# Projections with features first, undivided attention weights, and an earlier end of attention in a two-layer trunk on one core

## The chip, the core and the metric

One core of a Trainium2 chip runs the whole program. TensorE (PE) multiplies, VectorE (DVE), ScalarE (ACT) and GpSimd (POOL) work on tiles, and SyncE (SP) issues most of the DMAs. The metric is the time of the program on the device in microseconds, as the median of several runs. The profile comes from one more execution.

## The reference

The reference is a trunk of two layers over one sequence of 1024 tokens with 1024 features, in float32. Layer 0 mixes tokens with a diagonal state-space model, layer 1 with sparse attention; each mixer is followed by an MLP with squared ReLU (4096 hidden features), with a norm before and behind each.

```python
def dsa_mixer(h, w_in, w_out):
    proj = h @ w_in
    q, k, v, qi, ki, wi = jnp.split(proj, offs, axis=-1)   # 16 heads, 4 of k and v, 8 of the indexer, 64 wide
    q, k, qi, ki = (apply_rope(...) for each)
...
    rel = jax.nn.relu(jnp.einsum('bthd,bsd->bths', qi_blk, ki))
    score = jnp.einsum('bths,bth->bts', rel, wi_blk)       # causal
    _, idx = lax.top_k(score, 256)                         # per query, over 1024 keys
    att = jnp.einsum('btngd,btknd->btngk', qg, kg) * scale # chosen keys alone
    p = jax.nn.softmax(att, axis=-1)
    o = jnp.einsum('btngk,btknd->btngd', p, vg)
...
    return out @ w_out

def sq_relu_mlp(h, w1, w2):
    a = jax.nn.relu(h @ w1)
    return (a * a) @ w2
```

## The kernel before

**Layout and precision.** The residual stream lies with features on the partitions, 512 tokens (half a sequence, `hf` 0 or 1) along a row. To keep float32 accuracy each operand x is held as a rounded part `hi` and a rest `lo = x - hi`; `mm3` (lines 138 to 143) makes three matmuls of each product. A weight unit (`unit`, line 111) is a DMA of 512 KB into one of three raw buffers, two ScalarE copies (line 123) and two subtractions (line 124, one on VectorE, one on GpSimd).

**Passes.** The state-space layer comes first. Then four passes of the MLP follow, one for each layer and half, in `run` (line 1138): layer 0 half 0 alone; layer 0 half 1 with the attention of the first half beside it (`first`); layer 1 half 0 with the attention of the second half beside it (`second`); layer 1 half 1 alone. A pass has 64 units of 24 matmuls with 512 columns. After each unit `beside` (line 266) takes `self.per` steps from the generator beside it: 5 in the second pass, after a wait of 8 units, and `PER_B` in the third. Between the second and third passes stand the output projection of the first half, a residual and norm, and the indexer's projections of the second half, with nothing of the MLP beside them.

**Order.** The program order is that of the Python calls, but a planner orders the instructions of each engine by its own estimate of when each is needed; the side work has a higher priority. Tiles with the same tag share a fixed number of buffers: 22 tiles of 4 KB a partition under the tag `b`, three raw buffers `wr` for all weights. Since raw buffers are handed out in program order, the place of a `unit` call among the MLP's units is kept. The output projection of the second half (`att_out`, line 1057) is called once 58 units are through:

```python
            while self.units < HOLD_OUT:
                yield
            xo = self.att_in(self.od[1], "b")
            yield from self.att_out(xo, "b")
```

**Projections.** `proj` (line 725) multiplies with tokens on the output partitions: the stationary operand is 128 tokens of x, the moving one 256 features of a weight chunk. `heads` (line 768) rotates the result with `apply_rope` (line 752: line 760 over 512 elements, 762 and 763 over 256, then two additions on GpSimd), splits it into hi and lo, and later transposes each head of each 128 tokens (line 782), so that hi and lo of 64 features fill the 128 partitions. ScalarE copies them out (lines 798, 811) and queries go to DRAM as `qd` and `qi` (line 799), 256 KB at a time. Keys stay in four tiles of 256 tokens. `index` makes two chunks of indexer queries (the first half only its last 256 tokens), `projections` four chunks of queries, then keys, then values.

**Attention.** A block `i` is 128 queries. `topk` (line 902) finds each query's 256th largest score by 31 bit steps, whose small instructions on VectorE (lines 946 to 960) alternate with counts on VectorE or ScalarE (lines 916, 954). Per head, `weights` (line 996) multiplies queries and keys in pieces of 256 keys (line 1013), adds the mask and takes the maximum (line 1015), scales the maximum (line 1017), takes the exponential with its sum (line 1019), inverts the sum (line 1020) and multiplies all weights by it on GpSimd (line 1021). `outputs` (line 1025) transposes the weights, splits them and multiplies with the values; the result goes to DRAM as `od` (line 1050). `att_in` (line 1054) loads it and splits it.

## Time and profile before

| | before |
|---|---|
| median of 3 runs | 2305.07 us (2303.75 to 2305.22) |
| the profiled execution | 2311.69 us, its span 2309.9 us |
| mean granted clock of TensorE | 0.976 |
| busy: TensorE, VectorE, ScalarE, GpSimd | 95%, 63%, 48%, 39% |
| data moved by DMA | 258.48 MB, 112 GB/s |

The span runs from the first to the last instruction. Times in the rows count from its start. Matmuls overlap, so a mean duration of one is more than the time from one start to the next.

### The profile page before, as it was taken

Reading aid. Unit: us, or ns where it says so; the run is one execution under the profiler, and the core shown is the slowest. Engines: PE = TensorE matmul, PEld = TensorE weight load, DVE = VectorE, ACT = ScalarE, POOL = GpSimd, SP = SyncE. Lnnn points to the kernel's source line nnn. Section 1 sums busy time; section 2 is a strip of 40 time slices with the busy share of each in tenths; the row PEclk is TensorE's granted clock in tenths of the full one; section 3 lists DMA queues with packets and bytes.
Section 4 is the critical chain, followed back from the end, with each engine's and each line's share of the span. In section 5 each row is a group of like instructions: output and inputs, shape, how many; then the busy total and the mean of one; then the engine's idle time right before and its main releaser. Section 6 shows DMA issues by size and latency. Waiting matters only on the chain.

```text
span 2309.9 us, 31616 instructions
## 1 busy us (share of the span) xinstructions
PE 2194.5 (95%) x11392; PEld 1844.8 (80%) x11392; DVE 1451.1 (63%) x2977; ACT 1097.7 (48%) x2003; POOL 889.4 (39%) x712
## 2 busy tenths in 40 slices
PE   7899999999999999999998989899999998999996
PEld 3577778888889987888888878777889887788886
DVE  9465953333653598566695899999766748333335
ACT  4435643333454465455464565665455544323332
POOL 6004542222346443344346424344545425222223
PEclk9899999999999999999999999999999999999998
DMA  6112442333345544443445424332333245433331
GB/s 245 55 30 80 163 138 94 101 93 99 115 134 162 143 120 107 115 109 108 149 165 147 137 91 101 83 82 78 87 87 89 73 137 178 133 99 99 94 101 54
DMA packets 92989, 258.48 MB, mean 112 GB/s; under 512 B 10912, under 2 KB 23584, under 8 KB 92832
## 3 DMA queue, kind: packets, MB, share of 16 engines
q1 hardware_dynamic: 79072, 232.34, 31.5%
q0 software_dynamic: 12672, 23.07, 5.4%
q8 instruction: 90, 1.47, 0.3%
q10 hardware_dynamic: 1088, 1.05, 0.1%
q14 instruction: 67, 0.55, 0.1%
HBM read 222.73 MB, written 32.51 MB: 110 GB/s over the span
## 4 chain that ended last, share of the span: by engine, by line
PE 72%; DVE 15%; issue 5%; ACT 5%; POOL 1%; DMA 0%; SPq 0%; DVEq 0%; ACTq 0%; POOLq 0%
PE m L141 17%; PE m L143 17%; PE m L142 17%; PE p L1013 2%; PE p L141 2%; PE p L143 2%; PE p L142 2%; PE p L1034 2%; DVE wh L124 1%; DVE b L234 1%; PE p L1043 1%; DVE b L191 1%; PE p L1042 1%; PE p L883 1%; DVE acc L234 1%
## 5 line engine op out<-in xcount | busy, mean ns | idle before, releaser
L142 PE MATMUL m<-b,wh 128*128 128x512 f32 (+1 forms) x2208 | 860.7, 391 | 9.7 <-DVE b L191 7.2
L141 PE MATMUL m<-b,wh 128*128 128x512 f32 (+1 forms) x2208 | 862.7, 392 | 6.8 <-DVE ring L1017 2.5
L143 PE MATMUL m<-b,wh 128*128 128x512 f32 (+1 forms) x2208 | 860.0, 391 | 3.4 <-DVE wh L124 3.4
L124 POOL TENSOR_TENSOR wh<-wr,wh 128x512 fp32r<-128x512 f32 x318 | 467.1, 1470 | 1004.9 <-ACT wh L123 962.3
L123 ACT ACTIVATE wh<-wr 128x512 fp32r<-128x512 f32 x636 | 396.4, 628 | 486.8 <-PE m L143 406.0
L142 PEld LDWEIGHTS m<-b,wh 128*128 128x128 f32 x2208 | 419.0, 190 | 93.1 <-DVE b L191 9.7
L141 PEld LDWEIGHTS m<-b,wh 128*128 128x128 f32 x2208 | 418.9, 190 | 92.2 <-issue 4.2
L143 PEld LDWEIGHTS m<-b,wh 128*128 128x128 f32 x2208 | 418.7, 190 | 86.4 <-DVE wh L124 3.8
L124 DVE TENSOR_TENSOR wh<-wr,wh 128x512 fp32r<-128x512 f32 x318 | 269.3, 848 | 307.3 <-ACT wh L123 284.4
L318 DVE TENSOR_TENSOR acc<-acc,m 128x512 f32<-128x512 f32 x216 | 147.0, 681 | 145.4 <-PE m L143 143.8
L1021 POOL TENSOR_TENSOR s<-s,ring 128x128 f32<-128x128 f32 (+7 forms) x128 | 157.8, 1244 | 160.3 <-DVE ring L1020 141.6
L283 ACT ACTIVATE b<-m 128x512 f32<-128x512 f32 x128 | 76.3, 596 | 154.6 <-PE m L143 153.9
L141 PE MATMUL p<-wh,b 128*128 128x256 f32 x480 | 136.1, 289 | 3.0 <-ACT wh L123 3.0
L142 PE MATMUL p<-wh,b 128*128 128x256 f32 x480 | 137.2, 290 | 1.7 <-POOL wh L124 1.4
L132 DVE CAST b<-b 128x1024 fp32r<-128x1024 f32 x68 | 60.9, 896 | 122.0 <-ACT b L285 117.7
L143 PE MATMUL p<-wh,b 128*128 128x256 f32 x480 | 135.9, 287 | 0.0
L1038 ACT ACTIVATE pt<-p 128x512 fp32r<-128x512 f32 (+1 forms) x160 | 83.5, 554 | 92.1 <-PE p L1034 90.1
L1015 DVE CUSTOM_DVE_ANT_0 s<-p,nb 128x512 f32<-128x512 f32 (+3 forms) x192 | 100.2, 549 | 31.8 <-PE p L1013 30.3
L1019 ACT ACTIVATE s<-s,ring 128x128 f32<-128x128 f32 (+7 forms) x128 | 98.6, 772 | 44.4 <-DVE ring L1017 40.5
L1039 DVE TENSOR_TENSOR pt<-p,pt 128x512 fp32r<-128x512 f32 (+1 forms) x160 | 98.9, 630 | 29.0 <-ACT pt L1038 28.6
L954 ACT ACTIVATE junk<-b,ring 128x512 bf16<-128x512 f32 (+2 forms) x90 | 80.7, 897 | 73.6 <-DVE ring L950 68.0
L1013 PE MATMUL p<-kt,q 128*128 128x256 f32 x640 | 104.9, 293 | 5.0 <-DVE acc L318 2.4
(295 smaller groups left out, 3090.6 us busy)
## 6 DMA issues: line engine op xcount, KB each, us to landing
wr<-in_w_dram SPq DMA_DIRECT2D x256, 512.0 KB, 3.6
wr<-in_wa_dram SPq DMA_DIRECT2D x32, 512.0 KB, 3.7
q<-qd POOLq DMA_DIRECT2D x64, 256.0 KB, 5.4
ld<-hd SPq DMA_DIRECT2D x24, 512.0 KB, 6.3
hd<-b SPq DMA_DIRECT2D x16, 512.0 KB, 4.5
qd<-qt SPq DMA_DIRECT2D x32, 256.0 KB, 3.4
wr<-in_wao_dram SPq DMA_DIRECT2D x16, 512.0 KB, 3.6
q<-qi POOLq DMA_DIRECT2D x24, 256.0 KB, 5.1
```

The costliest lines, as they stand in the source:

```text
L123: nc.scalar.activation(hi, r, AF.Copy)
L124: (nc.gpsimd if h else nc.vector).tensor_sub(lo, r, hi.bitcast(F32))
L141: mm(ps, w[0], x[0], start=start, stop=False)
L142: mm(ps, w[0], x[1], start=False, stop=False)
L143: return mm(ps, w[1], x[0], start=False, stop=stop)
L318: nc.vector.tensor_add(acc[d][:, j], acc[d][:, j], ps)
L1013: nc.tensor.matmul(ps[:, 256 * e:256 * e + 256], qt[:, v, 2 * hp + k, :], self.K[2 * c + e][:, g, :], start=v == 0, stop=v == 1)
L1015: nc.vector.tensor_tensor_reduce(out=s[:, a:a + n], in0=ps[:, :n], in1=nb[:, a:a + n], scale=1.0, scalar=-BIG, op0=ALU.add, op1=ALU.max, a ...
L1019: nc.scalar.activation(s, s, AF.Exp, bias=ng[:, k, 0:1], scale=0.125, accum_out=sm[:, k, 0:1])
L1021: nc.gpsimd.tensor_tensor(s, s, rc[:, k, 0:1].to_broadcast([128, W]), op=ALU.mult)
L1038: nc.scalar.activation(ph[:, :nk], pt[:, :nk], AF.Copy)
L1039: nc.vector.tensor_sub(pl[:, :nk], pt[:, :nk], ph.bitcast(F32)[:, :nk])
```

## The change

- Queries and keys are projected with features on the output partitions (`proj_f`): the stationary operand is 128 features, the moving one 512 tokens. The weights are reordered while they are split, so that the first halves of four heads stand before their second halves (`unit(..., heads=True)`). `turned` rotates with tables that `att_r` makes once per half: copies of cosine and sine, eight transposes, copies back.
- `put_heads` sends hi and lo of each head to DRAM with eight DMAs per 128 features. Keys take the same way (`kd`) and come back as tiles of 512 keys; they are made ahead of the queries. `weights` multiplies with up to 512 keys at once.
- The weights are no longer divided by their sum. The negative scaled maximum comes from one instruction per piece; the sums of a block's 16 heads are inverted, turned and sent to DRAM (`norms`), and `att_in` multiplies the outputs by them, broadcast from DRAM over 64 partitions.
- `PER_B` becomes (7, 6, 7, 6, 6) and the output projection of the second half follows attention after two holds of one unit (`WAIT_OUT`) and no longer waits for unit 58.

```diff
-PER_B = (8, 6, 10, 10, 10)
+PER_B = (7, 6, 7, 6, 6)
-HOLD_OUT = 58
+WAIT_OUT = 1
...
-            nc.scalar.activation(hi, r, AF.Copy)
-            (nc.gpsimd if h else nc.vector).tensor_sub(lo, r, hi.bitcast(F32))
             out.append((hi, lo))
+            if heads:
+                rs = r.rearrange("p (k h e d) -> p e k h d", h=2, e=2, d=32)
+                his, los = [q.rearrange("p (k e h d) -> p e k h d", h=2, e=2, d=32) for q in (hi, lo)]
+                parts = [(his[:, e], los[:, e], rs[:, e]) for e in range(2)]
+            else:
+                parts = [(hi, lo, r)]
+            for ph, pl, pr in parts:
+                nc.scalar.activation(ph, pr, AF.Copy)
+                (nc.gpsimd if h else nc.vector).tensor_sub(pl, pr, ph.bitcast(F32))
...
+    def proj_f(self, x, chunk, n, body):
+        pss = [self.p1([128, 512]) for _ in range(2)]
+        for u in range(2):
+            ws = self.unit(self.a["wa"][chunk, u], heads=True)
+            for h in range(2):
+                for m in range(2):
+                    for kk in range(2):
+                        kt = 4 * u + 2 * h + kk
+                        w = [t[:, 256 * kk + 128 * m:256 * kk + 128 * m + 128] for t in ws[h]]
+                        self.mm3(pss[m][:, n], w, [q[:, kt % 2, n] for q in x[kt // 2]], kt == 0, kt == 7)
+                    if u and h:
+                        body(m, pss[m][:, n])
+                yield
...
+    def turned(self, ps, n):
+        nc = self.nc
+        cos, sin = self.turns[:, 0, n], self.turns[:, 1, n]
+        w = ps.shape[-1]
+        b = self.blk([128, 2, 512], tag="b")
+        t1, t2 = b[:, 0, :w], b[:, 1, :w]
+        nc.vector.tensor_mul(t1, ps, cos)
+        nc.vector.tensor_mul(t2[0:64], ps[64:128], sin[64:128])
+        nc.vector.tensor_mul(t2[64:128], ps[0:64], sin[0:64])
+        nc.gpsimd.tensor_add(t1, t1, t2)
+        st = self.blk([128, 2, 512], F32R, tag="b")[:, :, :w]
+        nc.scalar.activation(st[:, 0], t1, AF.Copy)
+        nc.gpsimd.tensor_sub(st[:, 1], t1, st.bitcast(F32)[:, 0])
+        return st.bitcast(F32)
+
+    def put_heads(self, st, dst, h0, t0=0):
+        for e in range(2):
+            for v in range(2):
+                for h in range(2):
+                    src = st[64 * e + 32 * h:64 * e + 32 * h + 32, v]
+                    self.nc.sync.dma_start(
+                        dst[t0:, 64 * v + 32 * e:64 * v + 32 * e + 32, h0 + h].rearrange("t d n -> d t n"),
+                        src.rearrange("d (t n) -> d t n", n=dst.shape[-1]))
+
+    def queries(self, hf, x, chunk, dst, g, n=slice(0, 512)):
+        yield from self.proj_f(x, chunk, n, lambda m, ps: self.put_heads(
+            self.turned(ps, n), dst[4 * hf:4 * hf + 4], 4 * g + 2 * m, n.start // 128))
 
     def keys(self, hf, x):
+        n = slice(0, 512)
+        def body(m, ps):
+            self.put_heads(self.turned(ps, n), self.kd[hf:hf + 1], 2 * m)
+            kt = self.blk([128, 2, 512], F32R, name="kt")
+            self.nc.sync.dma_start(kt.bitcast(F32), self.kd[hf, :, 2 * m:2 * m + 2])
+            self.K[hf].append(kt)
+        yield from self.proj_f(x, 0, n, body)
...
-        mx, ng, sm, rc = [self.small([128, 2, 2], F32, "sf", 16) for _ in range(4)]
         for k, s in enumerate(P):
+            least = None
             for c in range(nk):
                 a, n = 512 * c, min(512, W - 512 * c)
+                m = max(n, 256)
                 ps = self.p1([128, 512])
-                for e in range((n + 255) // 256):
-                    for v in range(2):
-                        nc.tensor.matmul(ps[:, 256 * e:256 * e + 256], qt[:, v, 2 * hp + k, :],
-                                         self.K[2 * c + e][:, g, :], start=v == 0, stop=v == 1)
-                nc.vector.tensor_tensor_reduce(out=s[:, a:a + n], in0=ps[:, :n], in1=nb[:, a:a + n], scale=1.0,
-                                               scalar=-BIG, op0=ALU.add, op1=ALU.max, accum_out=mx[:, k, c:c + 1])
-            nc.vector.tensor_scalar(ng[:, k, 0:1], mx[:, k, 0:1], mx[:, k, nk - 1:nk], -0.125,
-                                    op0=ALU.max, op1=ALU.mult)
-            nc.scalar.activation(s, s, AF.Exp, bias=ng[:, k, 0:1], scale=0.125, accum_out=sm[:, k, 0:1])
-            nc.vector.reciprocal(rc[:, k, 0:1], sm[:, k, 0:1])
-            nc.gpsimd.tensor_tensor(s, s, rc[:, k, 0:1].to_broadcast([128, W]), op=ALU.mult)
+                for v in range(2):
+                    nc.tensor.matmul(ps[:, :m], qt[:, v, 2 * hp + k, :], self.K[c][g // 2][:, g % 2, :m],
+                                     start=v == 0, stop=v == 1)
+                last, least = least, self.small([128, 1], F32)
+                nc.vector.tensor_tensor_reduce(out=s[:, a:a + n], in0=ps[:, :n], in1=nb[:, a:a + n], scale=-0.125,
+                                               scalar=last if c else BIG, op0=ALU.add, op1=ALU.min, accum_out=least)
+            h = 16 * (i % 4) + 4 * g + 2 * hp + k
+            nc.scalar.activation(s, s, AF.Exp, bias=least, scale=-1.0, accum_out=self.sums[:, h:h + 1])
             yield
...
+    def norms(self, i):
+        r = self.sums[:, 16 * (i % 4):16 * (i % 4) + 16]
+        nc.vector.reciprocal(r, r)
+        ps = self.p1([16, 128])
+        nc.tensor.transpose(ps, r, self.ident)
+        t = self.small([64, 256], F32, "ot", 2)[0:16, 0:128]
+        nc.scalar.activation(t, ps, AF.Copy)
+        nc.sync.dma_start(self.rd[i // 4][:, i % 4], t)
...
-        return [self.split(b(), [128, 2, 512], lo_pool=j % 2 == 1, tag=tag) for j, b in enumerate(self.load_h(od))]
+    def att_in(self, hf, tag, wait=0):
+        nc, got = self.nc, []
+        for j, b in enumerate(self.load_h(self.od[hf])):
+            hi, lo = [self.blk([128, 2, 512], F32R, tag=tag) for _ in range(2)]
+            x, rb = b(), lo.bitcast(F32)
+            for q in range(2):
+                h = 4 * (2 * (j // 2) + q) + 2 * (j % 2)
+                nc.sync.dma_start(rb[64 * q:64 * q + 64],
+                                  self.rd[hf][h:h + 2].rearrange("(o h) t n -> o (h t n)", o=1).to_broadcast([64, 1024]))
+            got.append((x, hi, lo))
+            if j == 2:
+                yield from self.hold(wait)
+        for x, hi, lo in got:
+            nc.vector.tensor_mul(x, x, lo.bitcast(F32))
+            nc.scalar.activation(hi, x, AF.Copy)
+            nc.vector.tensor_sub(lo, x, hi.bitcast(F32))
+        yield from self.hold(wait)
+        return [t[1:] for t in got]
...
     def projections(self, hf, x):
+        yield from self.keys(hf, x)
         for c in range(4):
             yield from self.queries(hf, x, 4 + c, self.qd, c)
-        yield from self.keys(hf, x)
         yield from self.values(hf, x)
-        self.flush()
...
-            while self.units < HOLD_OUT:
-                yield
-            xo = self.att_in(self.od[1], "b")
+            xo = yield from self.att_in(1, "b", WAIT_OUT)
             yield from self.att_out(xo, "b")
```

## Rows read from the trace of the kernel before

**Rows 1.** The page's head: busy us, share of the span, instructions.

```profile
span 2309.9 us, 31616 instructions
...
PE 2194.5 (95%) x11392; PEld 1844.8 (80%) x11392; DVE 1451.1 (63%) x2977; ACT 1097.7 (48%) x2003; POOL 889.4 (39%) x712
```

**Rows 2.** Busy us by stretch, then granted clock, DMA share, GB/s.

```profile
400.00:500.00 100.00, 100.00 (x443) 82.81 (x442) 33.68 (x45) 32.69 (x52) 23.18 (x18) 1.00 0.31 99
...
1300.00:1440.00 140.00, 129.44 (x699) 109.00 (x699) 130.66 (x288) 86.14 (x172) 49.51 (x47) 0.98 0.36 101
1440.00:1665.00 225.00, 208.91 (x1142) 176.26 (x1141) 202.12 (x520) 135.58 (x258) 98.45 (x76) 0.98 0.31 83
1665.00:1850.00 185.00, 183.94 (x1146) 164.58 (x1146) 127.51 (x300) 102.42 (x191) 91.89 (x61) 1.00 0.30 82
...
1900.00:1970.00 70.00, 62.74 (x271) 50.65 (x270) 58.80 (x63) 31.13 (x50) 36.09 (x21) 0.95 0.51 179
```

**Rows 3.** TensorE's waits over the span: us, times, longest.

```profile
PE p L782 <- POOL b L776: 7.6, 3, 3.2
```

**Rows 4.** TensorE's waits from 1850 to 1990.

```profile
PE c L178 <- DVE b L175: 4.0, 1, 4.0
PE m L142 <- DVE b L191: 3.2, 4, 1.0
```

**Rows 5.** Timeline of TensorE in a projection: start, us of one.

```profile
699.99 0.28 PE L143 MATMUL p<-wh,b 128*128 128x256 f32 x1
...
702.99 0.28 PE L141 MATMUL p<-wh,b 128*128 128x256 f32 x1
```

**Rows 6.** The chain that ended last: start, us, instructions.

```profile
727.07 1.75 PE p L782 x16
```

**Rows 7.** Costliest groups of TensorE by shape: count, busy us, mean ns.

```profile
L141 PE MATMUL p<-wh,b 128*128 128x256 f32 x480 | 136.1, 289 | 3.0 <-ACT wh L123 3.0
...
L1013 PE MATMUL p<-kt,q 128*128 128x256 f32 x640 | 104.9, 293 | 5.0 <-DVE acc L318 2.4 <-DVE ot L1049 2.2 <-DVE ring L1015 0.2
...
L782 PE MATMUL p<-con,b 128*128 128x128 f32 x208 | 31.6, 279 | 7.8 <-POOL b L776 7.6
```

**Rows 8.** Groups of VectorE by shape.

```profile
L135 DVE TENSOR_TENSOR b<-b,b 128x1024 fp32r<-128x1024 f32 x68 | 88.6, 1302 | 1.0
...
L950 DVE TENSOR_SCALAR ring<-ring 128x2 f32<-128x2 f32 x90 | 30.1, 334 | 1.9
...
L1017 DVE TENSOR_SCALAR ring<-ring 128x1 f32<-128x1 f32 x128 | 23.9, 201 | 0.1
...
L1020 DVE RECIPROCAL ring<-ring 128x1 f32<-128x1 f32 x128 | 19.1, 155 | 19.2 <-ACT s L1019 18.3
...
L760 DVE TENSOR_TENSOR b<-p,con 128x512 f32<-128x512 f32 x26 | 17.8, 684 | 8.6 <-PE p L143 8.6
...
L762 DVE TENSOR_TENSOR b<-p,con 128x256 f32<-128x256 f32 x26 | 10.7, 412 | 0.0
```

**Rows 9.** Costliest groups of the page, ScalarE and GpSimd.

```profile
L123 ACT ACTIVATE wh<-wr 128x512 fp32r<-128x512 f32 x636 | 396.4, 628 | 486.8 <-PE m L143 406.0
...
L1021 POOL TENSOR_TENSOR s<-s,ring 128x128 f32<-128x128 f32 (+7 forms) x128 | 157.8, 1244 | 160.3 <-DVE ring L1020 141.6
```

**Rows 10.** Line 950 by itself: ns min, median, max.

```profile
L950 DVE TENSOR_SCALAR ring<-ring x90: 145/169/1286, 1.7 to 1591.1; 128x2 f32<-128x2 f32 x90
```

**Rows 11.** Line 1050, stores of outputs by SP.

```profile
L1050 SPq DMA_DIRECT2D od<-ot x64: 507/513/712, 821.4 to 1846.3; - x64
...
DMA to landing us min/median/max: 2.0/2.2/7.0
```

**Rows 12.** Line 799, stores of queries by SP.

```profile
L799 SPq DMA_DIRECT2D qd<-qt x32: 319/326/992, 709.9 to 1338.7; - x32
```

**Rows 13.** Waits of SP's queue.

```profile
SPq L116 <- POOL wh L124: 854.7, 257, 23.3
...
SPq L799 <- ACT qt L798: 72.8, 26, 7.8
```

More of the change, by code (lines that the diff above doesn't have):

```diff
@@ L43, in bc_last, with finished @@
     return t.rearrange("p a (b o) -> p a b o", o=1).to_broadcast(shape)
+def finished(gen):
+    while True:
+        try:
+            next(gen)
+        except StopIteration as e:
+            return e.value
 class Trunk:
@@ L66, in __init__ @@
         self.n = 0
-        self.late = []
         self.scratch_tag = "b"
@@ L109, in small, with unit @@
         return t if dt == F32 else t.bitcast(dt)
-    def unit(self, src, last=False):
+    def unit(self, src, last=False, heads=False):
         nc = self.nc
@@ L788, in queries @@
-    def queries(self, hf, x, chunk, dst, g, tps=(0, 1)):
-        nc = self.nc
-        def body(tp, ps):
-            qt = []
-            def put(t, pt):
-                if not t:
-                    qt.append(self.blk([128, 2, 4, 128], F32R, name="qt"))
-                nc.scalar.activation(qt[0][:, t], pt, AF.Copy)
-                nc.sync.dma_start(dst[4 * hf + 2 * tp + t, :, 4 * g:4 * g + 4], qt[0].bitcast(F32)[:, t])
-            self.heads(hf, tp, ps, put)
-        yield from self.proj(x, chunk, tps, body)
@@ L1052, in outputs, with hold @@
         yield
-    def att_in(self, od, tag):
-        return [self.split(b(), [128, 2, 512], lo_pool=j % 2 == 1, tag=tag) for j, b in enumerate(self.load_h(od))]
+    def norms(self, i):
[7 more added lines that the diff above has]
+        nc.sync.dma_start(self.rd[i // 4][:, i % 4], t)
+    def hold(self, n):
+        end = self.units + n
+        while self.units < end:
+            yield
+    def att_in(self, hf, tag, wait=0):
[16 more added lines that the diff above has]
+        return [t[1:] for t in got]
     def att_out(self, x, ftag):
@@ L1078, in att_start @@
         self.qi = dp.tile([8, 128, 8, 128], F32, name="qi")
+        self.kd = dp.tile([2, 128, 4, 512], F32, name="kd")
         self.od = [dp.tile([4, 128, 2, 512], F32, name=f"od{h}") for h in range(2)]
+        self.rd = [dp.tile([16, 4, 128], F32, name=f"rd{h}") for h in range(2)]
     def att_r(self, hf, r):
@@ L1086, in att_r @@
             self.nc.vector.tensor_mul(t, t, r.rearrange("p (t o) -> p t o", o=1).to_broadcast([128, 4, 32]))
+        self.turns = self.blk([128, 2, 512], name="turns")
+        for k in range(2):
+            ps = self.p1([128, 4, 128])
+            c4 = self.blk([128, 4, 4, 32])
+            self.nc.scalar.activation(c4, bc_mid(self.rope[:, k, 4 * hf:4 * hf + 4], [128, 4, 4, 32]), AF.Copy)
+            for t in range(4):
+                self.nc.tensor.transpose(ps[:, t, :], c4[:, t].rearrange("p q d -> p (q d)"), self.ident)
+            ps = ps.rearrange("p t n -> p (t n)")
+            if k:
+                self.nc.scalar.activation(self.turns[0:64, k], ps[0:64], AF.Copy)
+                self.nc.scalar.activation(self.turns[64:128, k], ps[64:128], AF.Copy, scale=-1.0)
+            else:
+                self.nc.scalar.activation(self.turns[:, k], ps, AF.Copy)
     def index(self, hf, x):
@@ L1128, in attention_b @@
         sc = {}
+        self.new_sums(1)
         self.per = PER_B[2]
@@ L1171, in run @@
             pass
-        self.flush()
         def second():
```

40 lines of the change are left out of this document (11 added, 29 removed).

## Prediction

> **What bounds the kernel now.** I read the busy table first [rows 1]: TensorE works 2194.5 of 2309.9 us, so the kernel is bound by how many matmul columns pass, and 115.4 us are gaps. VectorE at 63% is no bound over the whole, but the table by stretches [rows 2] shows where it is one: from 1300 to 1665, while the top-k search runs beside projections and attention, VectorE is busy 93% and then 90% of the time, and TensorE idles 10.6 + 16.1 = 26.7 us there. From 1665 to 1850 (attention of the last blocks) TensorE is full again. Around 1900 to 1970 it idles 7.3 us. The waits of TensorE tell the reasons: transposes of rotated heads wait 7.6 us for GpSimd's low parts [rows 3], and near the end of the third MLP pass TensorE waits for the pre-norm of the other half (line 191, and line 175, its squares) [rows 4]. So the question is: which TensorE instructions go, and does the time come back where VectorE is nearly full?
>
> **Prices of TensorE.** What counts is the distance from start to start; the mean duration of one includes latency. In the pure MLP stretch 443 matmuls of 512 columns pass in 100 us [rows 2], 0.2257 us each. In the projections, 25 steps of 256 columns take 702.99 - 699.99 = 3.00 us [rows 5], 0.120 each. Sixteen transposes take 1.75 us [rows 6], 0.109 each. 384 columns lie halfway: 0.173, an estimate from these.
>
> **Projections.** A full chunk of 256 features is 96 matmuls of 256 columns (4 token blocks x 8 x 3); features first it is 48 of 512 (2 x 8 x 3): 11.52 against 10.83 us, 0.69 less. Full chunks: 4 + 1 in the first half, 2 + 4 + 1 in the second, 12 in all: 8.3 us. The two half chunks of the first indexer keep 48 of 256. With features on the partitions no head has to be turned: all 208 transposes of line 782 [rows 7] go, 208 x 0.109 = 22.7 us, and with them the 7.6 us of rows 3.
>
> **Scores of attention.** Line 1013 has 640 matmuls of 256 columns [rows 7], 76.8 us. With keys 512 wide there are 128 of 256 (blocks 0, 1 and the tails of 4, 5), 64 of 384 and 192 of 512: 15.4 + 11.1 + 43.3 = 69.8, so 7.0 us less.
>
> **Added on TensorE.** 16 transposes for the turned rope tables and 8 for the sums, 24 x 0.109 = 2.6 us. TensorE in sum: -8.3 - 22.7 - 7.0 + 2.6 = -35.4 us.
>
> **The other engines.** GpSimd loses the 128 divisions of line 1021, 157.8 us [rows 9]; it was 39% busy, so this alone is worth nothing. VectorE loses line 1017 (0.201) and the reciprocal 1020 (0.155) per head [rows 8], 0.356 x 128 = 45.6 us, 11.4 of it in attention of blocks 4 and 5, which runs in the tight stretch. The rotation costs VectorE more: 0.684 + 2 x 0.412 becomes 3 x 0.684 per tile (half the partitions, all 512 columns), +0.54, for ten tiles of the second projections +5.4 us. Splitting weights by halves of a head makes two instructions out of one on 56 half units: at most 56 x 0.628 us [rows 9] on ScalarE, 35 us on an engine 48% busy [rows 1], taken as hidden. The 52 copies of lines 798 and 811 go.
>
> There is one more way in which GpSimd's divisions may cost VectorE. The small bit steps of the search take 0.145 us at best, 0.169 in the median, and up to 1.286 [rows 10], about as long as a GpSimd instruction of line 1021 (mean 1.244 [rows 9]); with a mean of 0.334 [rows 8] over 90 of them the excess of this line is 90 x 0.165 = 15 us, whichever GpSimd instruction it stands behind, so what the divisions' removal frees lies between 0 and about 15 for such a line. The Trainium skill, SBUF - State Buffer, section Who interferes with whom, gives the mechanism: VectorE and GpSimd share a port pair which one of them holds for a whole instruction while the other blocks fully. The spread of [rows 10] agrees; by that rule the divisions' whole share of these waits comes back, as in the rival "freed" below.
>
> **The tight stretch.** VectorE loses 11.4 and gains 5.4, and the 10 side steps per MLP unit become 7 and then 6, so fewer attention steps press on it at once. Of the 26.7 us idle I take a third, 9 us; the bounds are 0 (TensorE's saved work only opens gaps) and 26.7.
>
> **The end of the third pass.** The output projection's weights come through the same three raw buffers as the MLP's, in program order, so it stood behind MLP unit 58 of 64; attention's last store goes out at 1846.3 [rows 11]. By steps: 74 steps of projections and search at 7 and 6 a unit, 16 at 7, 136 and 80 at 6 make 11.8 + 2.3 + 22.7 + 13.3 = 50 units, two holds of one unit and 8 steps more: about 53. The residual and pre-norm then have some 5 units x 24 x 0.2257 = 27 us more before their first reader. The waits on lines 191 and 175, 3.2 + 4.0 us [rows 4], go. The mean granted clock was 0.95 in that window [rows 2], so about a tenth of 70 us ran at 1.2 instead of 2.4 GHz after the gaps, at half pace: 3.5 us more. I take 10 in all; bounds 0 and 10.7.
>
> **Taking in attention's output.** Eight multiplications and four low parts moved from GpSimd are 12 x 1.302 [rows 8] = 15.6 us of VectorE. The second half's have slack; the first half's 7.8 us fall where the first pass ends, and TensorE has only MLP's last units to cover them: +3, between 0 and 15.6. The sums go out ahead of the last outputs, so their round trip lies under it.
>
> **SP's queue.** Eight DMAs of 64 KB per 128 features replace two of 256 KB: 224 puts instead of 44, plus 4 loads of keys, which wait for their own puts, 8 stores and 16 loads of sums. The nearest row is the store of outputs, also 64 KB in runs of 512 B: 0.513 us of SP each [rows 11]. A chunk needs 16 x 0.513 = 8.2, two weight loads at about 0.33 [rows 12] 0.65, and two waits for the rotated tile at 72.8 / 26 = 2.8 each [rows 13] 5.6: 14.5 us. Behind a waiting put stand the weight loads of the next unit. TensorE needs 10.8 us for a chunk alone; in the first half 4 steps of 5 per unit add 0.8 units (4.3) and make 15.1, in the second two steps per unit add two units and make 21.7. So SP sets the pace only in the second indexer, which has nothing beside it: 2 x 3.7 = 7.4, taken as +8; low bound 0, since SP waits 854.7 us for raw buffers [rows 13] and so runs ahead.
>
> **Sum.** -35.4 - 7.6 - 10 - 9 + 3 + 8 = -51.0 us. The profiled execution took 2311.69 us (span 2309.9), so it would take 2260.7. The median of the runs is 6.6 lower, 2305.07, which gives 2254.
>
> **Rivals.**
> "Pressed": attention has to end some 6 units earlier. VectorE had 460.3 us of work in 550 from 1300 to 1850 [rows 2]. It loses 64 x 0.356 = 22.8 and 6 units' MLP work (33.7 us per 18.5 units [rows 2], 11), gains 5.4: 432. The stretch shrinks by 6 x 5.42 = 32.5 and by TensorE's second-half savings (5 x 2.43 + 4.4 = 16.5) to 501. At 90% VectorE needs 480, which fits; at its present mean of 84% it needs 516, TensorE stands 15 us before the output projection with the MLP's units queued behind, and the 9 us of the tight stretch don't come: 2278. Chance 0.16.
> "Freed": without the divisions and with the thinner mix all 26.7 us come back, and SP and VectorE cost nothing new: -35.4 - 7.6 - 10 - 26.7 = -80: 2225. For it speaks the size of the divisions, 157.8 us [rows 9]; against it, that the low parts of the weights stay on GpSimd and VectorE's share was 93% [rows 2]. I spread it from 2222 to 2238. Chance 0.14.
> "Puts bind", the other side: a put has 512 runs to lay out over blocks and partitions and may take SP longer than a store of outputs. With x us of SP per chunk, and 0.33 for each MLP unit's weights, the loss is 2(x - 10.8) + 5(x + 0.3 - 15.1) + 5(x + 0.65 - 21.7); it eats 51 + 8 at x = 21.7, a put of 0.97 us. The longest put of before took 0.992 [rows 12], once; typical 64 KB stores lie between 0.507 and 0.712 [rows 11]. At 1.1 us, x = 23.9: 26 + 46 + 14 = 86 lost, 2332. The Trainium skill speaks against the change here: DMA: Bandwidth & Descriptors, section Rules for kernel authors, says to coalesce, since under 64 KB one pays mostly overhead; landing after 2.2 us [rows 11] agrees with overhead, but these land behind other work. Chance 0.06.
> "Work only": TensorE's 35 us come, every stall stays or is replaced (keys that arrive through DRAM late, buffers held longer by the keys and tables made first): 2270 to 2305. Chance 0.07, 0.03 of it within 0.2% of before.
>
> **Numbers.** Forecast case 0.57, 2238 to 2270, time 2254. The range leaves out the lower half of "freed" (0.07), "puts bind" (0.06) and the upper half of "work only" (0.035), under 0.2 together: 2230 to 2292. A difference under 0.2% can't be told from none here; faster by more than that 0.91, within it 0.03, slower 0.06.
>
> **What would show it.** No transposes in the projections and 48 matmuls of 512 per chunk, 0.226 apart; TensorE busy near 2160. If the idle of the search stretch stays near 27 us the thinner mix did nothing. Puts near 0.5 us on SP, and no TensorE wait on weight conversions in the second indexer. The output projection near unit 53 with no wait for attention ahead of it, and no wait on the pre-norm at the start of the last pass. I am wrong if SP's puts or attention's end show up as gaps of TensorE over 20 us, or if VectorE's share falls so far that the search no longer matters.

## The result, and the profile after

The changed kernel takes 2285.74 us (median, 2281.77 to 2287.54) where the kernel before, run beside it, took 2305.14: a ratio of 0.9917 (95% interval 0.9903 to 0.9931), 19.4 us less. The forecast was 51 less. The sign and the range hold; the size is well under half.

The head of the page of the changed kernel answers to [rows 1]:

```profile
span 2285.6 us, 29529 instructions
...
PE 2166.6 (95%) x10376; PEld 1785.5 (78%) x10376; DVE 1436.7 (63%) x2775; ACT 1083.0 (47%) x2027; POOL 701.8 (31%) x588
```

The span is 24.3 us shorter. TensorE's busy time fell by 27.9, but its idle time rose from 115.4 to 119.0, where it was to fall. The mean granted clock went from 0.976 to 0.971. Between the levels of 2.4 and 1.2 GHz (1.0 and 0.5) that is 2 x 0.024 x 2309.9 = 111 us at the low level before and 2 x 0.029 x 2285.6 = 133 after; at half pace 22 us more cost 11. So TensorE has, by this estimate, 27.9 + 11 = 39 us less to do at full clock, against 35.4 forecast, and gives 11 back through the clock and 3.6 through gaps.

The stretches of the changed kernel (columns: stretch, length, busy us of each engine with its instructions, granted clock, DMA share, GB/s), to set beside [rows 2]:

```profile
1300.00:1440.00 140.00, 120.26 (x536) 97.42 (x535) 130.41 (x274) 73.32 (x153) 51.08 (x43) 0.94 0.39 102
1440.00:1650.00 210.00, 206.42 (x1104) 175.59 (x1104) 181.54 (x488) 141.46 (x270) 49.80 (x46) 1.00 0.35 92
...
1450.00:1600.00 150.00, 149.00 (x816) 128.04 (x814) 133.00 (x390) 112.86 (x217) 31.62 (x30) 1.00 0.35 93
...
1720.00:1800.00 80.00, 67.25 (x409) 56.95 (x408) 57.25 (x123) 49.73 (x91) 3.66 (x5) 0.91 0.34 90
1785.00:1794.00 9.00, 1.39 (x4) 0.84 (x3) 3.14 (x4) 1.68 (x3) 0.00 (x0) 0.70 0.78 193
```

The search of blocks 6 and 7 (1450 to 1600) is now full: 1.0 us idle of 150, and 3.6 up to 1650, where [rows 2] had 16.1 up to 1665 (both ends lie 57 us behind the search's last bit step). The projections ahead of it idle 19.7 of 140 at clock 0.94 (10.6 at 0.98 before). The end of attention, 1720 to 1800, full before, idles 12.8, most of it in the last stretch shown. The waits of TensorE from 1670 to 1930 (us in total, times, longest) name that gap:

```profile
PE m L157 <- ACT b L1108: 7.6, 1, 7.6
PE c L194 <- POOL b L191: 3.3, 1, 3.3
```

Line 1108 is ScalarE's conversion of attention's output in `att_in`. The timelines of the changed kernel, SP's queue first, then VectorE (start, duration; in brackets the idle time before and its releaser), show what it stands behind:

```profile
1784.19 0.32 SPq L1085 DMA_DIRECT2D rd<-ot  x1
1784.76 0.51 SPq L1072 DMA_DIRECT2D od<-ot  x1
1785.64 2.41 SPq L1101 DMA_DIRECT2D b<-rd  x4
1788.14 0.54 SPq L1072 DMA_DIRECT2D od<-ot  x1
1788.79 1.18 SPq L1101 DMA_DIRECT2D b<-rd  x2
```

```profile
1785.53 0.42 DVE L1071 TENSOR_TENSOR ot<-p,ol 64x256 f32<-64x256 f32 x1 [0.80 <-ACT ol L1069]
1790.32 1.22 DVE L1107 TENSOR_TENSOR ld<-ld,b 128x1024 f32<-128x1024 f32 x1 [4.38 <-DMA b<-rd]
```

The last block's sums leave at 1784.19, 0.6 us ahead of the last outputs but one. All eight loads of sums (`b<-rd`) come behind them, the first multiplication waits for the first load until 1790.3, and TensorE for the multiplication. In the kernel before, two of the four inputs were loaded at 1812.8 and 1816.5, well ahead of attention's last store at 1846.3 [rows 11], and the projection began on them at 1844.1. The changed kernel loads two of its inputs early too, at 1766.2 and 1770.8; what they lack is the sums.

A second place is where the tables are turned. TensorE's timeline in the changed kernel, between the second and third passes, and the clock just after (windows, columns as above):

```profile
1163.36 0.39 PE L159 MATMUL m<-b,wh 128*128 128x512 f32 x1
1165.22 0.66 PE L1153 MATMUL p<-con,b 128*128 128x128 f32 x4 [1.46 <-ACT b L1151]
1167.32 1.12 PE L1153 MATMUL p<-con,b 128*128 128x128 f32 x4 [1.44 <-ACT b L1151]
```

```profile
1163.00:1167.00 4.00, 1.41 (x8) 0.71 (x6) 2.23 (x9) 3.25 (x9) 0.97 (x2) 1.00 0.28 112
1168.00:1172.00 4.00, 4.00 (x15) 3.23 (x14) 0.50 (x1) 1.18 (x2) 0.00 (x0) 0.66 0.48 135
```

Eight transposes of 0.11 us each bring two gaps of 1.46 and 1.44 us, since each four wait for ScalarE's copy of a table (line 1151). The first copy waits for the pre-norm's factors, which VectorE multiplies in at 1164.2 (line 1144), and the second stands behind other copies on ScalarE. The indexer's key matmuls, which need neither, are queued behind them. The granted clock is 0.66 right behind the gaps.

The puts, in the view of their line (ns min, median, max), were cheaper than the 0.513 us that I took from [rows 11]:

```profile
L815 SPq DMA_DIRECT2D qd<-b x128: 302/430/2214, 723.8 to 1359.2; - x128
```

### The profile page after: what moved, and what is told of

It is laid out like the page before. It is cut to its first block, busy times and chain, and to the rows that moved or that the text cites. A ratio compares the mean times of both kernels' runs of the same rounds, so it can differ in the third digit from the quotient of the medians.

```text
span 2285.6 us, 29529 instructions
## 1 busy us (share of the span) xinstructions
PE 2166.6 (95%) x10376; PEld 1785.5 (78%) x10376; DVE 1436.7 (63%) x2775; ACT 1083.0 (47%) x2027; POOL 701.8 (31%) x588
## 4 chain that ended last, share of the span: by engine, by line
PE 73%; DVE 15%; ACT 6%; issue 4%; DMA 1%; POOL 1%; SPq 0%; ACTq 0%; DVEq 0%; POOLq 0%
PE m L158 18%; PE m L157 18%; PE m L159 18%; PE p L1036 2%; PE p L1056 2%; PE p L157 2%; PE p L159 2%; PE p L158 2%; DVE wh L141 2%; PE p L1064 1%; DVE b L250 1%; PE p L1065 1%; ACT junk L974 1%; DVE b L207 1%; PE m L611 1%
## 5 line engine op out<-in xcount | busy, mean ns | idle before, releaser
L141 POOL TENSOR_TENSOR wh<-wr,wh 128x512 fp32r<-128x512 f32 (+1 forms) x346 | 448.7, 1302 | 1281.6 <-ACT wh L140 1261.6
L140 ACT ACTIVATE wh<-wr 128x512 fp32r<-128x512 f32 (+1 forms) x692 | 400.0, 592 | 503.2 <-PE m L159 413.9
L141 DVE TENSOR_TENSOR wh<-wr,wh 128x512 fp32r<-128x512 f32 (+1 forms) x346 | 273.4, 797 | 296.8 <-ACT wh L140 283.2
L159 PE MATMUL p<-b,wh 128*128 128x512 f32 (+1 forms) x304 | 116.1, 391 | 8.4 <-DVE wh L141 8.4
L157 PE MATMUL p<-b,wh 128*128 128x512 f32 (+1 forms) x304 | 115.8, 398 | 5.7 <-ACT b L721 3.4
L158 PE MATMUL p<-b,wh 128*128 128x512 f32 (+1 forms) x304 | 117.3, 391 | 0.0
L1043 ACT ACTIVATE s<-s,ring 128x128 f32<-128x128 f32 (+7 forms) x128 | 98.6, 772 | 36.6 <-DVE ring L1040 35.4
L1036 PE MATMUL p<-kt,q 128*128 128x512 f32 (+2 forms) x384 | 100.2, 365 | 1.5 <-DVE pt L1061 1.2
L1056 PE MATMUL p<-con,s 128*128 128x128 f32 x576 | 93.1, 273 | 0.0
L1040 DVE CUSTOM_DVE_ANT_0 s<-p,nb 128x512 f32<-128x512 f32 (+3 forms) x128 | 72.6, 582 | 25.4 <-PE p L1036 25.2
```

Source lines behind the costliest of these rows:

```text
L140: nc.scalar.activation(ph, pr, AF.Copy)
L141: (nc.gpsimd if h else nc.vector).tensor_sub(pl, pr, ph.bitcast(F32))
L157: mm(ps, w[0], x[0], start=start, stop=False)
L158: mm(ps, w[0], x[1], start=False, stop=False)
L159: return mm(ps, w[1], x[0], start=False, stop=stop)
L1036: nc.tensor.matmul(ps[:, :m], qt[:, v, 2 * hp + k, :], self.K[c][g // 2][:, g % 2, :m], start=v == 0, stop=v == 1)
```

## The experiments

Ratios are to the kernel before, run beside each kernel on the same chip.

| run | base | edit | median us | ratio, 95% interval |
|---|---|---|---|---|
| tokens_first | changed | projections and keys as before | 2294.96 | 0.9961 (0.9946 to 0.9975) |
| divide | changed | division on GpSimd as before | 2297.78 | 0.9972 (0.9963 to 0.9981) |
| pace_before | changed | pacing as before | 2285.49 | 0.9919 (0.9904 to 0.9934) |
| hold58 | changed | output projection behind unit 58, not 52 | 2294.01 | 0.9953 (0.9937 to 0.9969) |
| hold55 | changed | the same, behind 55 | 2280.70 | 0.9894 (0.9879 to 0.9910) |
| per_old | changed | old steps per unit, no hold (unit 37) | 2312.80 | 1.0035 (1.0022 to 1.0049) |
| permuted | changed | weight columns reordered in memory | 2286.88 | 0.9924 (0.9906 to 0.9943) |
| puts_late | changed | puts behind the next weight loads | 2286.75 | 0.9923 (0.9908 to 0.9937) |
| tables_late | changed | tables turned later | 2273.56 | 0.9867 (0.9850 to 0.9885) |
| sums_half | changed | sums sent in two halves | 2274.88 | 0.9867 (0.9846 to 0.9888) |
| late55 | tables_late | and unit 55 | 2273.25 | 0.9865 (0.9851 to 0.9878) |
| thin_first | tables_late | 6 steps per unit at first | 2273.73 | 0.9864 (0.9851 to 0.9877) |
| rot_less | tables_late | no sine part | 2276.44 | 0.9879 (0.9864 to 0.9895) |
| first_index | tables_late | second indexer at side priority | 2287.59 | 0.9928 (0.9916 to 0.9941) |
| both | tables_late | and sums_half | 2265.89 | 0.9837 (0.9821 to 0.9852) |
| both55 | both | and unit 55 | 2271.57 | 0.9859 (0.9843 to 0.9874) |
| both_tokens | both | projections and keys as before | 2291.45 | 0.9934 (0.9917 to 0.9951) |
| both_pace | both | pacing as before | 2276.84 | 0.9877 (0.9864 to 0.9890) |

### What each part is worth in the changed kernel

`tokens_first` undoes the projections:

```diff
-    def proj_f ... turned ... put_heads
+    def heads ... queries, keys with transposes, as before
-                    nc.tensor.matmul(ps[:, :m], qt[...], self.K[c][g // 2][:, g % 2, :m], ...)
+                        nc.tensor.matmul(ps[:, 256 * e:256 * e + 256], qt[...], self.K[c][e][:, g, :], ...)
```

> The changed kernel with the projections of before (tokens on the output partitions, heads transposed on TensorE, keys 256 wide, no tables, no sends by 64 KB); joined division and steps per unit stay. TensorE's work by the rows of before is 33 to 36 us more. Theory 'VectorE' (the rotation with 3 x 512 elements and the split by halves of a head load VectorE in the stretches beside the projections and give about 15 us back as gaps): 2300 to 2308 us. If the projections' saving came through whole: 2318 to 2325. If it was lost whole: 2283 to 2290.

`divide` undoes the division joined in:

```diff
+            nc.vector.reciprocal(rc, self.sums[:, h:h + 1])
+            nc.gpsimd.tensor_tensor(s, s, rc.to_broadcast([128, W]), op=ALU.mult)
...
-            nc.vector.tensor_mul(x, x, lo.bitcast(F32))
```

> The changed kernel with the division of attention's weights by their sums put back on GpSimd, head by head, and no multiplication of the outputs. Theory 'chain': the way of the outputs is shorter again, 2278 to 2284 us. Theory 'port' (GpSimd's divisions hold up VectorE's two-input and small instructions during the search): the idle time of TensorE in the search stretch from 1440 to 1600 comes back, about 10 us: 2292 to 2300.

`pace_before` undoes the pacing:

```diff
-PER_B = (7, 6, 7, 6, 6)
+PER_B = (8, 6, 10, 10, 10)
+            while self.units < 56:
+                yield
             xo = yield from self.att_in(1, "b", WAIT_OUT)
```

> The changed kernel with the side steps per unit of before (8, 6, 10, 10, 10) and the second attention output projection held to unit 58 as before: projections and division stay, the spreading of attention over the third pass is undone. Theory 'pacing is worth what its parts showed': against the changed kernel it loses the cover at the search (idle 1.0 to about 10 us) and gets the pre-norm wait at the start of the last pass, 2292 to 2300. Rival 'pacing is worth nothing by itself': with attention ended early TensorE waits nowhere for it, 2283 to 2289.

Undone one at a time, the projections cost 9 us (they save 38 us of matmuls by the forecast's own terms, 8.3 + 22.7 + 7.0), the division 12, the pacing nothing. In `divide` the gaps of the search come back. Its stretch of the search, by windows:

```profile
1450.00:1590.00 140.00, 126.89 (x654) 105.15 (x652) 132.91 (x356) 92.28 (x177) 54.10 (x45) 0.96 0.28 79
```

13.1 us idle of 140 at clock 0.96, where the changed kernel idles 1.0 of 150. So the idle of the search belonged to the divisions. The small bit steps of the search show it on VectorE, here one of their four lines in the kernel before, the changed kernel and `divide` (busy us, mean ns):

```profile
L959 DVE TENSOR_TENSOR ring<-ring,con 128x2 int32<-128x2 f32 x93 | 27.3, 294 | 13.0 <-ACT junk L954 10.3
L979 DVE TENSOR_TENSOR ring<-ring,con 128x2 int32<-128x2 f32 x93 | 18.0, 194 | 12.7 <-ACT junk L974 10.0
L979 DVE TENSOR_TENSOR ring<-ring,con 128x2 int32<-128x2 f32 x93 | 30.5, 328 | 13.0 <-ACT junk L974 10.6
```

The four lines together take 107.8, 83.9 and 103.0 us. `divide` also brings back the 128 inversions (19.1 us of VectorE); which of the two holds TensorE was not separated. And no sums travel in `divide`: at the end of its third pass TensorE waits for no conversion of attention's output. So the 12 us are net of that gap; what the division costs without it was not run. The pacing's result missed its expectation: 2285.49 is the rival's value.

### Where the output projection stands

`hold58`, `hold55` and `per_old` move it alone or with the old steps.

```diff
+            while self.units < 56:     # hold58; 53 in hold55
+                yield
             xo = yield from self.att_in(1, "b", WAIT_OUT)
...
-PER_B = (7, 6, 7, 6, 6)
+PER_B = (8, 6, 10, 10, 10)             # per_old, without a hold
```

> The changed kernel with one thing added: the output projection of the second half waits again, so that its weights come behind MLP unit 58 of the third pass (the loads of attention's output may start at unit 56). Theory 'queue' (the changed kernel loses time because the output projection's weights stand at unit 53 and attention ends later than that, so that TensorE has no MLP left from 1720 to 1800): the idle 12.8 us and about 7 us at the lower clock level there come back, the wait for the pre-norm ahead of the fourth pass returns in part (7 us): 2270 to 2278 us. Theory 'chain' (TensorE waits there for the longer way of the outputs, with the sums sent through DRAM and the multiplication): the wait of 7.6 us on the split of attention's output stays, wherever the output projection stands: 2284 to 2292.

> The changed kernel with the steps per unit of before (8, 6, 10, 10, 10) and no hold beyond the two units: the calls of attention end near unit 35 and the output projection's weights come at about unit 37. Theory 'queue': 16 more MLP units, 87 us of TensorE's work, are held behind attention; most of it can't hide, 2330 to 2370 us. Theory 'chain': the place doesn't matter, 2280 to 2292.

> The changed kernel with the second attention output projection held until 53 units have been issued, so it stands behind unit 55 of 64 in place of 52 (changed kernel) or 58 (the held run). Theory 'two gaps that trade': at 52 TensorE waits for attention's end (10.8 us idle plus low clock), at 58 for the pre-norm at the start of the last pass (6.6 us plus 17 us of low clock); in between each is covered, 2277 to 2282. Rival 'linear': every unit later costs a little, so half way between the two measured times, 2288 to 2291.

The place matters: 27 us are lost at unit 37 with the old steps. At 58 it costs 8, and 55 may be a little better than 52 (the intervals overlap). But no place closes the gap. The waits of TensorE in `hold58` near the end of its third pass:

```profile
PE m L157 <- ACT b L1108: 8.1, 1, 8.1
PE m L157 <- ACT b L206: 7.3, 1, 7.3
PE m L158 <- DVE b L151: 3.9, 1, 3.9
PE c L194 <- DVE b L191: 2.0, 1, 2.0
```

The wait for line 1108 is there as at unit 52, and TensorE waits besides for line 206, the pre-norm at the start of the last pass. At units 37, 52, 55 and 58 the projection waits 7.6 to 8.1 us for line 1108, so the wait does not hang on units. That it hangs on attention's last sums is tested below by `sums_half`.

### Suspects that were none

`permuted` stores the weight columns in split order, so that a half unit is again one instruction of 512; `puts_late` keeps the puts in a list that is emptied after the next chunk's weight loads.

```diff
-            ws = self.unit(self.a["wa"][chunk, u], heads=True)
+            ws = self.unit(self.a["wa"][chunk, u])           # permuted; columns reordered in the layout
...
+            self.late.append(lambda: self.put_heads(st, ...))  # puts_late
+            if u: self.flush()                               # behind the two weight loads of the next chunk
```

> The changed kernel with the columns of the 32 q and k weight blocks already stored in the order that the split by halves of a head produces, so each half unit is one conversion of 512 columns on ScalarE and one low part on VectorE or GpSimd, as it was before the change; everything else is the changed kernel. Theory 'split': the 256-wide pairs (about 0.83 us each on VectorE where one of 512 takes 0.79) are why weights come late to TensorE (waits of 3.9 us in the middle stretch and 4.0 us in the projections); without them those waits and the low clock behind them go, 2272 to 2279. Rival 'hidden': the extra instructions lie beside other work, as the prediction took them, and the time stays within 3 us of the changed kernel, 2283 to 2289.

> The changed kernel with each tile's eight 64 KB puts moved behind the two weight loads of the next projection chunk in SP's order (the key loads with them). Theory 'queue': weight loads that stand behind puts waiting for GpSimd's low part are what starves TensorE in the second indexer (gap of 3.87 us at 1208.9 and the low clock for 10.2 us after it) and in the second projections; with the puts moved away 2273 to 2280. Rival 'conversion': weights arrive early enough and the gaps come from VectorE and GpSimd converting them late; then no change, 2283 to 2289, and the 3.87 us gap stays.

Neither moved the time, so the split by halves of heads costs nothing here and SP's order is not what starves the second indexer. Its gap stays with the puts out of the way (waits of TensorE from 1190 to 1230 in `puts_late`, where line 142 is the low part of a weight):

```profile
PE p L160 <- DVE wh L142: 7.7, 1, 7.7
```

`rot_less` (on late tables) leaves out two of three rotation instructions:

```diff
-        nc.vector.tensor_mul(t2[0:64], ps[64:128], sin[64:128])
-        nc.vector.tensor_mul(t2[64:128], ps[0:64], sin[0:64])
-        nc.gpsimd.tensor_add(t1, t1, t2)
+        nc.gpsimd.tensor_add(t1, t1, t1)
```

> Rope tables late, and the two half-width sine multiplications of each rotated tile left out (GpSimd adds the cosine part to itself), so q and k are rotated wrongly; VectorE does 1.37 us less per tile, 5.5 us in the second indexer and 13.7 us in the second projections. Theory 'rotation on VectorE is what eats the projections' gain': idle plus low clock of the middle and the projections stretch fall by 10 us or more and the time goes to 2258 to 2265. Rival 'other VectorE work and shared buffers': the gaps stay, 2270 to 2275.

VectorE's busy time falls by 35 us (1434.0 in `tables_late`, 1398.6 here), and nothing is gained: the rotation's price was rightly small.

### The two places

`tables_late` calls the table part of `att_r` from `index_keys`, behind the key matmuls in program order:

```diff
+        self.tables(hf)
         ki = self.apply_rope(pt[:, :, 56:120] ...)
```

> The changed kernel with the turned rope tables made inside the indexer's key projection, after the attention output projection has been issued, not straight behind the pre-norm. Theory 'tables': their transposes stand in TensorE's order where it already waits for the pre-norm (2.05 us), add two gaps of 1.46 and 1.44 us at 1164 and 1166, and it is this row of gaps that pulls the clock to 0.5 for 3.4 us at 1168; without them the middle stretch is 5 to 9 us shorter, 2277 to 2281. Rival 'same gaps': the gaps only move to the key projection, and the time is 2283 to 2288.

12.2 us, more than expected. TensorE's waits between the passes (1100 to 1280) in `tables_late` no longer name the tables:

```profile
PE p L159 <- DVE wh L141: 6.0, 1, 6.0
PE c L194 <- DVE b L191: 2.0, 1, 2.0
PE c L236 <- DVE ring L169: 1.8, 1, 1.8
PE p L875 <- POOL b L872: 1.6, 1, 1.6
```

By its page (busy 2157.3 of 2270.6, clock 0.975) it idles 113.3 us, 5.7 less, and runs 113.5 us at the low level, 19 less, worth 9.5: nearly two thirds of the 15.0 us of its span came back as clock, not as closed gaps. The first half's tables had the same place after the first pass. Matched instruction by instruction, `tables_late` is level with the changed kernel up to the first tables (at 638 us of the latter), 5.2 us ahead up to the second (1165), 10.9 behind them (1195) and 14.9 at the end: 10.9 us arise at the two places of the tables, the rest in the projections that follow. One profile differs from the next in its clock too, so the shares are rough.

`sums_half` sends heads 0 to 7 of a block once they are done, the rest at the end, and takes in the first two inputs without the last sums:

```diff
-                        if behind[0] < i:
-                            self.norms(behind[0])
+                        if behind[:3] in ((i, 1, 1), (i - 1, 3, 1)):
+                            self.norms(*behind[:2])
...
-            if j == 2:
-                yield from self.hold(wait)
+            if j % 2:
+                yield from self.hold(wait)
+                for x, hi, lo in got[j - 1:]:   # multiply and split these two
```

> The changed kernel with the sums of a block sent in two halves (heads 0 to 7 once they are done, heads 8 to 15 at the end), and the first two of the four inputs of the output projection taken in as soon as theirs are there; 8 small transposes and stores more. Theory 'last sums hold all four': each input needs the sums of the last block, sent only at the very end, so the whole taking-in (load, multiplication, conversion) stands open on TensorE as the gap of 7.6 us at 1785, with low clock behind it; with the halves apart the gap falls under 2 us and the time to 2272 to 2279. Rival 'attention ends too late': at unit 52 the MLP units are used up anyway, the gap stays above 5 us and the time at 2283 to 2289.

11 us, as expected of the theory. The waits of TensorE in `sums_half`, from 1720 to 1990:

```profile
PE c L194 <- POOL b L191: 3.3, 1, 3.3
PE m L158 <- DVE b L1110: 2.4, 1, 2.4
PE m L157 <- ACT b L1109: 1.9, 1, 1.9
```

The gap of 7.6 us is now 1.9 and 2.4. From 1780 to 1810 TensorE idles 2.4 us at clock 0.89 here, and 8.4 at 0.83 in the changed kernel.

`both` joins the two edits.

> Rope tables late and sums sent in halves. Theory 'two places that add': 12 us from the tables and 7 to 13 from the gap ahead of the output projection: 2260 to 2267. Rival 'one fixed end' (as the later place and the late tables did not add): 2270 to 2275.

At 2265.89 it is the best of all kernels run, 38 us under before and 20 under the changed kernel; 12.2 and 10.9 add to 23, of which 20 came.

### What else was tried around them

> Both edits that helped, together: rope tables made inside the indexer's key projection, and the second attention output projection behind unit 55. Theory 'two separate places': the middle stretch and the end of the third pass don't touch, so their gains of 12.2 and 5.0 us add: 2267 to 2271. Rival 'same time twice': a shorter middle only brings the attention to its end earlier or later against the MLP units, and one gain swallows the other: 2272 to 2276.

> Rope tables late, and 6 side steps per MLP unit in place of 7 beside the second projections and the scores of blocks 4 and 5 (about 1.8 units more there, so that the attention output projection stands behind unit 54 by itself). Theory 'VectorE presses': with VectorE busy 93% of the stretch around 1280 to 1440, fewer side steps per unit take idle (17.4 us) and low clock (13.7 us) out of it, on top of the later place: 2262 to 2268. Rival 'only the place counts': as the run with unit 55 and late tables, 2267 to 2272, with the idle of that stretch as it was.

```diff
-PER_B = (7, 6, 7, 6, 6)
+PER_B = (6, 6, 7, 6, 6)     # thin_first
```

> Rope tables late, sums in halves, and the output projection behind unit 55 in place of 52. Theory 'cover': with the first inputs early the units moved ahead of the projection lie under the last block's stores and loads, 2258 to 2263. Rival 'place no longer matters': within 3 us of the run with both edits at unit 52.

With the tables late neither a later place nor a thinner first mix gives anything, and with both edits unit 55 costs 5.7 us by the medians (the intervals just overlap).

`first_index` puts the second indexer ahead of the first half's norms:

```diff
+        with self.tc.high_priority(offset=PRIORITY):
             for _ in self.index(1, x1):
```

> Rope tables late, and the second indexer issued at the side work's priority, so its weight conversions and rotations stand ahead of the first half's post-norm and pre-norm on VectorE, GpSimd and ScalarE. Theory 'order on VectorE': the weights' low parts (1.15 us each there for 256 columns) stand behind the pre-norm's and make the 6.0 us gap and 6.8 us of low clock at 1196; with the indexer ahead 2264 to 2270. Rival 'the pre-norm is then what is late': the gap moves to the first units of the MLP pass, 2271 to 2277.

14 us slower than `tables_late`, worse than either theory said. The waits of TensorE from 1130 to 1450:

```profile
PE m L157 <- ACT b L206: 5.6, 1, 5.6
PE p L904 <- ACT r L905: 5.2, 1, 5.2
```

Now the pass waits for its pre-norm (line 206), as the rival had it, and besides it the scores wait. The gap in the indexer stays unmended. Where it comes from shows in VectorE's timeline in `tables_late` and in the view of line 141 in that stretch (1185 to 1206; ns min, median, max):

```profile
1197.08 2.55 DVE L207 SCALAR_TENSOR_TENSOR b<-b,con,b 128x512 fp32r<-128x512 f32 x2
1199.55 4.62 DVE L141 TENSOR_TENSOR wh<-wr,wh 128x256 fp32r<-128x256 f32 x4
1204.10 0.68 DVE L800 TENSOR_TENSOR b<-p,turns 128x512 f32<-128x512 f32 x1
```

```profile
L141 DVE TENSOR_TENSOR wh<-wr,wh x5: 941/1476/1775, 1193.3 to 1202.7; 128x256 fp32r<-128x256 f32 x4, 128x512 fp32r<-128x512 f32 x1
```

Four low parts of 256 columns take 4.62 us there, 1.15 each, where the shortest in that kernel takes 0.41; the windows give GpSimd 15.05 busy of 18 us beside them:

```profile
1188.00:1206.00 18.00, 12.05 (x46) 9.47 (x45) 17.85 (x20) 3.73 (x10) 15.05 (x11) 0.84 0.47 129
```

### Are the forecast gains there once the two places are mended?

`both_tokens` and `both_pace` undo the projections and the pacing in `both`, with the diffs of `tokens_first` and `pace_before`.

> The kernel with sums in halves, but q/k projections tokens first and keys 256 wide, as before the change (no turned tables then). Theory 'the tables ate the projections' gain': undoing them costs 9 us in the changed kernel and must cost 9 + 12 = 21 us here, 2284 to 2290. Rival 'a fixed end': as later place and late tables did not add, most of the saving is still lost elsewhere, 2270 to 2278.

> The kernel with late tables and sums in halves, side steps per unit as before (8, 6, 10, 10, 10) and the output projection held to unit 58. Theory 'pacing counts once the gap is gone': before's pre-norm wait at the start of the last pass and the denser search come back, 2272 to 2280. Rival 'pacing is worth nothing': 2263 to 2269, as undoing it changed nothing in the changed kernel.

The projections are now worth 25.6 us by the medians, 22 by the ratios (9 in the changed kernel), and the pacing 11 (nothing there). `both_pace` brings back the waits of [rows 4] to the tenth, in the waits of TensorE from 1780 to 1960:

```profile
PE c L194 <- DVE b L191: 4.0, 1, 4.0
PE m L158 <- DVE b L207: 3.2, 4, 1.0
```

## Why the prediction was right in sign and wrong in size

**TensorE's work: right.** The prices held: 39 us less at full clock, the estimate above, against 35.4. The idle of the search went from 16.1 to 3.6 us.

**"Added on TensorE", 2.6 us: the first step that failed.** 24 transposes were costed by their duration. The 16 of the tables wait on TensorE for copies that wait for the pre-norm, ahead of matmuls that could run, and the clock is low behind the gaps. Moving them alone gave 12.2 us. I asked what the edit adds, not what TensorE waits for at that place.

**"Attention's output taken in", +3 us: the second.** I put the cost on the first half and wrote that the second half's sums go out ahead of the last outputs, so that their round trip lies under it. They go out 0.6 us ahead of the last outputs but one and 4.0 ahead of the last, and every one of the four inputs needs them, since a block's 16 sums travel together. The second half's share, put at nothing, measured 11 us (`sums_half`). The first half's, put at 3, did not show as a wait of TensorE: it waits for line 1108 once in the whole span.

**The end of the third pass, -10 us: right in size, hidden.** The pacing removed the waits of [rows 4] (the one on line 175 was for the squares of the post-norm, which VectorE adds, and not the pre-norm's as I read it). A wait of 3.3 us for the pre-norm's squares on GpSimd (line 191, above) and the gap of the second step took their place; undone in the changed kernel it is worth nothing, undone in `both` 11. This is close to the rival "pressed", which saw TensorE stand idle before the output projection, but for another reason: not attention ending too late for its units (no place of the projection helped), but its sums.

**The tight stretch, -9 us.** The idle left the search (16.1 to 3.6 us) and grew in the projections ahead of it (10.6 to 19.7), so the net was 3. The search's part is due to the divisions, by `divide`, not to the thinner mix (`pace_before` kept it away: 2.9 us of 130 idle there). Line 950 was a poor sign of it: of its 17 instructions above 0.4 us only 3 stood beside a division, the others beside weights' low parts and rotations on GpSimd, and it gave back 5 of the 15 us named (30.1 to 25.0). The projections' part was not removed by less rotation, by another weight layout or by a thinner first mix: in those runs the stretch (1285 to 1425) idles 16 to 21 us of 140, with VectorE busy 129 to 130. Its cause stays open.

**SP's queue, +8 us: wrong cause, similar size.** A put took 0.43 us (its 64 KB in runs of 512 B are 128 runs, not the 512 that "puts bind" counted), and moving the puts changed nothing. The second indexer does lose 4 to 8 us in one gap, by VectorE's late low parts. The long instructions of [rows 10] had shown the pattern: VectorE beside a busy GpSimd. The Trainium skill, SBUF — State Buffer, section Who interferes with whom, says that a VectorE instruction with two inputs in SBUF contends with GpSimd's reads, and that one with a single SBUF input does not, outside its two-port modes. The rows agree: line 141, with two, stretched from 0.41 to 1.15 us, and line 800, which reads PSUM and one table, stayed at 0.68. That the contention makes the gap was not tested by itself.

**The transposes' wait, -7.6 us,** went with the transposes, as forecast, but gaps of the same kind (conversions late for a projection) took its place: 8.4 us for VectorE's low parts (line 141) in the projections' matmuls of the changed kernel, 3.8 before (line 124).

**The sum.** Mending the two failed steps gives 2265.89, inside the forecast case's own 2238 to 2270. For the 12 us that are still missing against 2254 no run shows the cause; in `both` TensorE waits 13.2 us for line 141 in the projections' matmuls, and the clock of their stretch is 0.95. As it stands, the result lies where the rival "work only" had it (2270 to 2305, chance 0.07): TensorE's work came and its stalls were replaced, though by the tables and the sums and not by the late keys and held buffers that it named.

## What to carry to other kernels

Price an added instruction by what it waits for at its place in the queue, above all on the engine that bounds the kernel: sixteen small transposes cost 12 us, seven times their own 1.75. Where a result is scaled late by something that is complete only at the end, send that something in the pieces in which it is used, or the last piece holds all. And undo a part both in the kernel as it is and in one with the suspected hole mended: the pacing was worth nothing in the one and 11 us in the other.

## What the runs showed of the hardware

Over the 4 us behind gaps of 1.46 and 1.44 us the granted clock was 0.66, and in `tables_late` more of the gain came through the clock (19 us less at the low level, worth 9.5) than through idle time (5.7 us less). VectorE's low parts beside a busy GpSimd took 1.15 us in place of 0.41, and its multiplications that read PSUM no longer than elsewhere (0.68). Of the 56 low parts of 256 columns in `tables_late`, the 31 with no GpSimd instruction beside them took 0.41 to 0.43 us, and the 11 wholly beside one 0.96 in the median. A put of 64 KB by SP (0.43 us) was cheaper than a store of outputs of the same size (0.51).
